# Attention's values projected first in each layer, and attention begun half a stretch earlier beside the last pairs' scan

## The chip, the cores and the metric

The kernel runs on one core of a Trainium2 chip. The metric is the device time of one execution in microseconds (us); the median of three runs is given. A profile is of one execution, whose span runs from its first to its last instruction.

## The reference

Two layers of a bidirectional encoder, 256 tokens of width 2048 in float32. Each layer normalises its input, makes one wide projection, and feeds two groups: a bidirectional RWKV-7 scan (16 heads of 64, one scan forward and one backward) and windowed attention (16 query heads, 4 key and value heads of 64, with rotary positions and a sink). Both are gated, joined, projected back and added to the input.

```python
h = rms_norm(x, norm_g[l])
proj = h @ w_in[l]
rw_in, g_rw, q, k_at, v_at, g_at = split(proj)
rw_in = bidir_token_shift(rw_in, shift_mu[l])
r, k, v, xw, xa = split(rw_in)          # xw, xa: low-rank inputs of decay and in-context rate
y_rw = rwkv7_branch(r, k, v, xw, xa, ...)   # both directions summed, normed, plus a bonus term
y_at = window_attention(rope(q), rope(k_at), v_at, sink[l])
mix = concat([y_rw * silu(g_rw), y_at * silu(g_at)])
x = x + mix @ w_out[l]
# after both layers: rms_norm(x, final_g)
```

## The kernel before

**The stream.** Every projection runs as a queue of *steps*, in an order written out by hand (class `Stream`, `S.add` and `S.run`). A step is three matmuls of 128x128 against 128x256 (lines 311 to 313): weights and activations are each split into a high part (float32r) and the rest, and high by high, high by low and low by high are summed. The activations of a layer lie in `XH` and `XL`, 16 slices (`k`) of 128 rows; `x_split` makes a slice's two parts, one on ScalarE (L203), one on VectorE (L204). A weight tile of 512 KB (`raw`, three buffers) serves eight steps; it is loaded by SP's queue (L233) and split into `hi` on ScalarE (L241) and `lo` on VectorE (L243), two buffers of each, asked for two steps before its first step. A projection's 128 columns are 16 steps into one accumulator (`pm`); two such buffers exist (`ps_main`). When it is full, its `evac` function is emitted; `S.later(n, f)` emits `f` n steps later.

**Order of the stream in a layer, 864 steps.** The low-rank inputs `xw` and `xa` (32 steps), eight pairs of RWKV heads with k, v, r and gate (512), attention's values (32: `v_step`, tokens as the stationary side, two accumulators of 128 tokens by 256 columns, both in `ps_main`), attention's two key tiles (32), and queries and gates of eight head pairs (256). After that come 256 steps of the output projection.

**Stretches.** `window(64, ...)` emits 64 steps in 11 groups; before each group it lets the generators that are listed for this group go one piece further: `scan_p` (preparation), `scan_i` (a triangular inverse), `scan_b` (the chain over four chunks) of the pairs at that lag, `setup_` (constants, the rotary sine and cosine; layer 0 only) and `attend`. So the pieces' small matmuls stand between stream steps in TensorE's order, which is the program's. The other engines' instructions are ordered by a scheduler at compile time, by priorities. Stretch w works on pairs w to w-4. Each layer has 13 stretches (numbered from 0); 32 steps run ahead of the first of them, in layer 0 while x arrives (one step for each slice of x, then 16 more) and in layer 1 behind layer 0's output projection.

**Attention.** `attend` has 16 pieces and a rest: `scores(j)` (12 matmuls into `pscr`, softmax on VectorE and ScalarE), `flip(j)` (transposes of the probabilities), `values(j)`. Table `ATT` says in which groups of the last three stretches a piece stands; the last of these has no scan.

**Buffers touched.** `S` of scores: tag `mv`, or `ge` for j = 2. Keys' low halves: tags `kd` and `kkr`. `VA` holds the values, and in layer 0's setup the rotary angles. `FR` (tag `s0b`) is scan_p's. `lead` does not exist yet; the low-rank projections use `ps_main` (in layer 0 the first uses a bank of the pair pool `ps_w`).

Of the kernel before, what the change touches and what calls it, by code (L numbers as in the profile page):

```python
# [9 lines left out]
F32 = mybir.dt.float32  # L10
# [11 lines left out]
T = 256  # L22
# [24 lines left out]
STAGE_I = (list(range(SLOTS)), [0, 1, 2, 3, 4])  # L47
STAGE_B = (list(range(5, SLOTS)), [i for i in range(SLOTS) if i != 7], [7])
ATT = [
    [3, 9],  # L50
    [1, 3, 5, 6, 8, 10],
    [0, 2, 4, 5, 6, 8, 9, 10],
]

ROT = {0: [2, 3], 1: [], 7: [2, 5, 7], 8: [1, 3], 9: []}
# [78 lines left out]
def hybrid_trunk_kernel(ctx, tc, xT, wi, wv, wo, par, fing, dup, iup, sink, pos, cst, out):  # L134
# [21 lines left out]
    def wbank(name):  # L156
        return wpair(name)[:, 0]
# [160 lines left out]
        S.add(ld[0], [step(k) for k in range(8)])  # L318
        S.add(ld[1], [step(k) for k in range(8, 16)], lambda: evac(box[0]))

    first_w = [wrp.tile([128, 1024], F32, tag="raw", name="raw") for _ in range(2)]
    G0 = cp.tile([128, NKT], F32, name="G0")
    X0 = Rows("s0", F32, "X0")
    SY.dma_start(out=first_w[0][:, 0:512], in_=wi[0, 0, 0, :, 0:512])
    SY.dma_start(out=G0, in_=par[0, :, P_NG : P_NG + NKT])
    for a, b in ((0, 2), (2, 4), (4, 8), (8, 12), (12, 16)):
        SY.dma_start(out=X0[:, a:b, :], in_=xT[:, a:b, :])
        if a == 0:
            SY.dma_start(out=first_w[0][:, 512:1024], in_=wi[0, 0, 0, :, 512:1024])
        if a == 4:  # L330
            SY.dma_start(out=first_w[1], in_=wi[0, 0, 1])
    mhalf = cp.tile([128, 4], F32, name="mhalf")
    V.memset(mhalf, -0.5)

# [12 lines left out]
    def setup():  # L347
        posi = st("t1", [T], I32, bufs=3)
        SY.dma_start(out=posi, in_=pos.to_broadcast([128, T]))
        SY.dma_start(out=FG, in_=fing)  # L350
        SY.dma_start(out=SK, in_=sink.to_broadcast([128, DEPTH * 16]))
        cin = st("mv", [C_N - C_KEEP], bufs=3)
        SY.dma_start(out=cin, in_=cst[:, C_KEEP:C_N])
        for l in range(DEPTH):
            s = DP[:, l, 0:NSH]
            V.tensor_tensor(s, PR[:, l, P_MU0 : P_MU0 + NSH], PR[:, l, P_MU1 : P_MU1 + NSH], op=ALU.add)
            V.tensor_scalar(s, s, -1.0, 1.0, op0=ALU.mult, op1=ALU.add)
            h = DP[:, l, NSH : NSH + 8]
            V.tensor_scalar(h, PR[:, l, P_KA : P_KA + 8], 0.5, None, op0=ALU.mult)
            V.tensor_scalar(DP[:, l, NSH + 8 : NSH + 16], h, -1.0, 1.0, op0=ALU.mult, op1=ALU.add)  # L360
            V.tensor_scalar(DP[:, l, NSH + 16 : NSH + 32], PR[:, l, P_A0 : P_A0 + 16], 0.5, None, op0=ALU.mult)
        V.tensor_scalar(SK, SK, 8.0, None, op0=ALU.mult)
        yield

        V.tensor_copy(
            LV.rearrange("p l s (n x) -> p (l s) n x", x=32),
            cin[:, 512 : 512 + 64 * NL].rearrange("p (n x) -> p n x", x=32).unsqueeze(2).to_broadcast([128, 2 * NL, NC, 32]),
        )
        V.memset(MSK, 1.0)
        V.memset(MSK[:, :, 0:1], 0.0)  # L370
        V.tensor_copy(band, cin[:, 0:512])
        A.activation(BONES, ones, AF.Copy, scale=0.0)
        for r in half:
            A.activation(BONES[r, r], ones[r, r], AF.Copy)
        V.tensor_copy(EYE, cin[:, 512 + 64 * NL : 576 + 64 * NL])
        V.tensor_scalar(NEYE, EYE, -1.0, None, op0=ALU.mult)
        V.tensor_scalar(EYE2, EYE, 2.0, None, op0=ALU.mult)
        yield

        AN = st("VA", [2, T])  # L380
        ang, nn = AN[:, 0], AN[:, 1]
        V.tensor_copy(ang, posi)
        yield
        PV.tensor_scalar(ang, ang, C[:, C_OFF["inv"] : C_OFF["inv"] + 1], None, op0=ALU.mult)
        yield

        def reduce_by(dst, src, period, bits, shift):
            PV.tensor_scalar(nn, src, 1.0 / period, shift, op0=ALU.mult, op1=ALU.add)
            yield
            PV.tensor_scalar(nn, nn, MAGIC, MAGIC, op0=ALU.add, op1=ALU.subtract)  # L390
            yield
            cur = src
            for p in split_const(period, bits, 4):
                PV.scalar_tensor_tensor(dst, nn, -p, cur, op0=ALU.mult, op1=ALU.add)
                cur = dst
                yield

        two_pi = 2.0 * np.pi
        yield from reduce_by(ang, ang, two_pi * 4096.0, 7, 0.0)
        for dst, shift, add in ((SIN, 0.0, 0.0), (COS, 0.25, np.pi / 2)):  # L400
            yield from reduce_by(dst, ang, two_pi, 11, shift)
            if add:
                PV.tensor_scalar(dst, dst, float(add), None, op0=ALU.add)
            PV.tensor_scalar(dst, dst, PI_IN, -PI_IN, op0=ALU.min, op1=ALU.max)
            yield
        for dst in (SIN, COS):
            PA.activation(dst, dst, AF.Sin)
        yield
        PV.tensor_scalar(SIN, SIN, C[:, C_OFF["sgn"] : C_OFF["sgn"] + 1], None, op0=ALU.mult)
        yield  # L410
# [30 lines left out]
    def queue_inputs(l):  # L441
# [53 lines left out]
            A.activation(hi, x[0:rows], AF.Copy)  # L495
            V.tensor_tensor(lo, x[0:rows], hi.bitcast(F32), op=ALU.subtract)

        if l == 0:

            inproj(0, lambda pm: S.later(29, lambda: xw_evac(pm)), raws=first_w, bank=lambda: wbank("pm")[:, 0:T])  # L500
            inproj(1, lambda pm: S.later(13, lambda: xa_evac(pm)))
        else:
            inproj(0, xw_evac)
            inproj(1, xa_evac)


        L.ts = [dict() for _ in range(NP)]
# [60 lines left out]

            return evac

        pvs = []

        def v_step(kk, b):
            def f(w):
                if not pvs:
                    pvs.extend(ps_main.tile([128, T], F32, tag="m", name="pva") for _ in range(2))
                k = kk % 4
                wh, wl = (x[:, k * 256 : (k + 1) * 256] for x in w)
                tb = slice(b * 128, (b + 1) * 128)
                PE.matmul(pvs[b], L.XH[:, kk, tb], wh, start=(kk == 0), stop=False)  # L580
                PE.matmul(pvs[b], L.XH[:, kk, tb], wl, start=False, stop=False)
                PE.matmul(pvs[b], L.XL[:, kk, tb], wh, start=False, stop=(kk == 15))

            return f

        def v_evac():
            L.VA = st("VA", [2, 256])
            with tc.high_priority(offset=PRIO_B):
                A.activation(L.VA[:, 0, :], pvs[0], AF.Copy, scale=L.norm.rt[:, 0:1])
                V.tensor_scalar(L.VA[:, 1, :], pvs[1], L.norm.rt[:, 1:2], None, op0=ALU.mult)  # L590

        for qt in range(4):
            S.add(
                lambda qt=qt: wsplit(wload(wv[l, qt])),
                [v_step(qt * 4 + k, b) for k in range(4) for b in range(2)],
                v_evac if qt == 3 else None,
            )

        def k_place(m):
            def place():  # L600
                if m == 0:
                    L.KA = [st("KA", [2, T], F32R), [st(n, [T], F32R) for n in ("kd", "kkr")]]
                return L.KA[0][:, m, :], L.KA[1][m]

            return place
# [68 lines left out]
    def layer(l):  # L674
# [399 lines left out]
        def scores(j):  # L1074
            m, g = divmod(j, 4)
            t = L.tq[j]
            Sc = t["S"] = st("ge", [2, 2, 264], bufs=2) if j == 2 else st("mv", [2, 2, 264], bufs=3)
            ps2 = wpair("pscr")
            pss = [ps2[:, h] for h in range(2)]
            qh, ql = t["q"]  # L1080
# [49 lines left out]
        def attend():  # L1130

            scores(0)
            yield
            flip(0)
            scores(1)
            yield
            for x in (MH, ML):
                x.more()
            for j in range(8):
                values(j)  # L1140
                if j < 6:
                    scores(j + 2)
                yield
                if j < 7:
                    flip(j + 1)
                    yield

        for w in range(NP + 2):
            window(64, *scans(w), *([(setup_, ROT.get(w, [2, 5, 9, 9]))] if l == 0 else []))
        att = attend()  # L1150
        window(64, *scans(NP + 2), (att, ATT[0]))
        window(64, *scans(NP + 3), (att, ATT[1]))
        window(64, (att, ATT[2]))
        for _ in att:
            pass

# [10 lines left out]
    L0.XH, L0.XL = Rows("s2", F32R, "XH"), Rows("s3", F32R, "XL")  # L1167
    for k in range(NKT):
        x_split(L0.XH, L0.XL, X0[:, k, :], k, 0)
        S.run(1)  # L1170
    ACC = st("mv", [4 * T], bufs=3)
    for q in range(4):
        x4 = X0[:, 4 * q : 4 * q + 4, :].rearrange("p k t -> p (k t)")
# [2 lines left out]
        else:  # L1176
            SQ = st("mv", [4 * T], bufs=3)
            PA.activation(SQ, x4, AF.Square)
            PV.tensor_tensor(ACC, ACC, SQ, op=ALU.add)
    S.later(20, lambda: L0.norm.add([ACC[:, i * T : (i + 1) * T] for i in range(4)]))  # L1180
    S.later(27, lambda: L0.norm.spread())
    S.run(8)
    SY.dma_start(out=C, in_=cst[:, 0:C_KEEP])
    SY.dma_start(out=PR, in_=par.rearrange("l p n -> p l n"))
    setup_ = setup()
    next(setup_)
    S.run(8)
    for l in range(DEPTH):
        queue_output(l)
        if l + 1 < DEPTH:  # L1190
            queue_inputs(l + 1)
        layer(l)
        S.run(NKT * 16)
        if l + 1 < DEPTH:
            S.run(32)
    end.norm.add(end.sums)
    end.norm.spread()
    X2 = layers[-1].X2
# [86 lines left out]
```

## Time and profile before

| what | value |
|---|---|
| median of 3 runs | 1171.13 us (1170.99 to 1171.94) |
| profiled execution | 1172.07 us, span 1170.3 us, granted clock 0.994 |
| TensorE busy | 1147.2 us (98%) |
| VectorE busy | 907.0 us (78%) |
| ScalarE busy | 786.4 us (67%) |
| DMA | 166.63 MB, mean 142 GB/s |

The page's lines give for an engine its busy time; a timeline row has start, duration, engine, line, operation, `out<-in` tiles, shape, count, and in brackets the engine's idle time before it with what ended it. PE is TensorE, PEld its weight load, DVE VectorE, ACT ScalarE, POOL GpSimd, SP the engine that issues the DMAs. Matmuls are pipelined: their starts say more than their durations.

### The profile page before, as it was taken

To read this page: it belongs to the slowest core of one execution; us is meant where nothing else is said; L and a number is where in the kernel's file an instruction comes from. 1 tells how busy PE (TensorE), PEld (TensorE's weight loads), DVE (VectorE), ACT (ScalarE), POOL (GpSimd) and SP (SyncE) were. 2 spreads that over 40 slices of the span, in tenths; PEclk is the share of its full clock that TensorE was granted. 3 is DMA by queue.
4 is the path that set the end of the run, shared out by engine and by line. 5 is a ranking of instruction groups with operands and counts; after the bars stand their busy time and mean duration, and the time that the engine had idled before them with its cause. 6 is when DMAs were issued, how large, how long until landed. Compare 5 with 4: busy or idle time off the path is not lost.

```text
span 1170.3 us, 38097 instructions
## 1 busy us (share of the span) xinstructions
PE 1147.2 (98%) x16151; PEld 1073.1 (92%) x16151; DVE 907.0 (78%) x2017; ACT 786.4 (67%) x1987; POOL 21.8 (2%) x23
## 2 busy tenths in 40 slices
PE   8999999999999999999999999999999999999996
PEld 6998999999899989899999899999999999899996
DVE  6889978888877677766678888978887767786554
ACT  6667877786876666645556677876886666675552
POOL 0000000000000000000000000000000000000000
PEclk9999999999999999999999999999999999999998
DMA  7544333233333433477655443333333343336663
GB/s 261 167 153 133 125 105 130 100 105 112 105 125 116 135 118 128 141 228 241 210 184 173 134 135 116 111 113 121 98 111 111 123 143 114 118 132 203 207 191 120
DMA packets 60410, 166.63 MB, mean 142 GB/s; under 512 B 7728, under 2 KB 22736, under 8 KB 60240
## 3 DMA queue, kind: packets, MB, share of 16 engines
q1 hardware_dynamic: 60240, 164.21, 43.2%
q8 instruction: 126, 2.06, 0.7%
q14 instruction: 44, 0.36, 0.1%
HBM read 157.37 MB, written 4.19 MB: 138 GB/s over the span
## 4 chain that ended last, share of the span: by engine, by line
PE 75%; issue 13%; DVE 6%; ACT 3%; DMA 1%; SPq 0%; POOL 0%; POOLq 0%; DVEq 0%; ACTq 0%
PE pm L311 19%; PE pm L313 16%; PE pm L312 16%; PE pg L833 3%; DVE lo L243 2%; PE pcc L996 2%; PE pcc L1024 2%; PE pd L940 1%; PE py L1008 1%; PE py L981 1%; PE pq L931 1%; PE pcc L1014 1%; ACT hi L241 1%; DMA raw<-wi 1%; PE pza L691 1%
## 5 line engine op out<-in xcount | busy, mean ns | idle before, releaser
L243 DVE TENSOR_TENSOR lo<-raw,hi 128x512 fp32r<-128x512 f32 x560 | 372.4, 687 | 112.8 <-ACT hi L241 103.7
L241 ACT ACTIVATE hi<-raw 128x512 fp32r<-128x512 f32 x560 | 329.7, 625 | 167.6 <-PE pm L312 96.3
L311 PE MATMUL pm<-XHa,hi 128*128 128x256 f32 x832 | 246.9, 297 | 1.4 <-ACT XHa L203 0.8
L311 PE MATMUL pm<-XHb,hi 128*128 128x256 f32 x832 | 242.9, 292 | 0.2 <-ACT hi L241 0.2
L313 PE MATMUL pm<-XHb,lo 128*128 128x256 f32 x832 | 233.6, 281 | 2.4 <-DVE lo L243 2.4
L313 PE MATMUL pm<-XHa,lo 128*128 128x256 f32 x832 | 234.3, 282 | 1.2 <-DVE lo L243 1.0
L312 PE MATMUL pm<-XLa,hi 128*128 128x256 f32 x832 | 234.3, 282 | 0.5 <-DVE XLa L204 0.3
L312 PE MATMUL pm<-XLb,hi 128*128 128x256 f32 x832 | 233.5, 281 | 0.4 <-DVE XLb L204 0.4
L311 PEld LDWEIGHTS pm<-XHa,hi 128*128 128x128 f32 x832 | 157.2, 189 | 13.8 <-issue 3.2
L311 PEld LDWEIGHTS pm<-XHb,hi 128*128 128x128 f32 x832 | 156.5, 188 | 5.9 <-ACT hi L241 0.4
L313 PEld LDWEIGHTS pm<-XHa,lo 128*128 128x128 f32 x832 | 157.3, 189 | 2.5 <-DVE lo L243 2.5
L313 PEld LDWEIGHTS pm<-XHb,lo 128*128 128x128 f32 x832 | 156.6, 188 | 3.2 <-DVE lo L243 3.2
L312 PEld LDWEIGHTS pm<-XLa,hi 128*128 128x128 f32 x832 | 157.5, 189 | 1.1 <-DVE XLa L204 1.1
L312 PEld LDWEIGHTS pm<-XLb,hi 128*128 128x128 f32 x832 | 156.7, 188 | 0.6 <-DVE XLb L204 0.6
L1019 ACT ACTIVATE suv<-pcc 64x128 f32<-64x128 f32 x128 | 34.7, 271 | 71.0 <-PE pcc L1017 47.3
L311 PE MATMUL pm<-MHa,hi 128*128 128x256 f32 x256 | 72.0, 281 | 0.0
L313 PE MATMUL pm<-MHa,lo 128*128 128x256 f32 x256 | 71.7, 280 | 0.2 <-DVE lo L243 0.2
L312 PE MATMUL pm<-MLb,hi 128*128 128x256 f32 x256 | 71.6, 280 | 0.0
L313 PE MATMUL pm<-MHb,lo 128*128 128x256 f32 x256 | 71.6, 280 | 0.0
L312 PE MATMUL pm<-MLa,hi 128*128 128x256 f32 x256 | 71.6, 280 | 0.0
L311 PE MATMUL pm<-MHb,hi 128*128 128x256 f32 x256 | 71.6, 280 | 0.0
L311 PEld LDWEIGHTS pm<-MHa,hi 128*128 128x128 f32 x256 | 48.1, 188 | 0.9 <-issue 0.8
(293 smaller groups left out, 2325.1 us busy)
## 6 DMA issues: line engine op xcount, KB each, us to landing
raw<-wi SPq DMA_DIRECT2D x207, 512.0 KB
raw<-wo SPq DMA_DIRECT2D x64, 512.0 KB
raw<-wv SPq DMA_DIRECT2D x8, 512.0 KB
rrot<-u SPq DMA_DIRECT2D x80, 32.0 KB
vg<-xT SPq DMA_DIRECT2D x16, 128.0 KB
xd<-vg SPq DMA_DIRECT2D x16, 128.0 KB
vg<-xd SPq DMA_DIRECT2D x16, 128.0 KB
g<-dup SPq DMA_DIRECT2D x16, 97.0 KB
```

The source lines that it names most:

```text
L241: A.activation(hi[:, q], raw[:, q], AF.Copy)
L243: V.tensor_tensor(lo[:, q], raw[:, q], hi[:, q].bitcast(F32), op=ALU.subtract)
L311: PE.matmul(pm, wh, rh[:, kk, :], start=(kk == 0), stop=False)
L312: PE.matmul(pm, wh, rl[:, kk, :], start=False, stop=False)
L313: PE.matmul(pm, wl, rh[:, kk, :], start=False, stop=(kk == 15))
L691: PE.matmul(o, w[0], x[0], start=True, stop=False)
L833: PE.matmul(pg[:, h, c * 128 : (c + 1) * 128], BK[half[h], d, c, 1 - h : 3 - h, :].rearrange("p s j -> p (s j)"), MV[half[h], d, c].rearra ...
L931: PE.matmul(narrow(pq[:, d], h ^ d, c), hq(AB, d, c, h), sub(TC, h, d, c, d * b), start=True, stop=True)
L940: PE.matmul(narrow(pd[:, d], h, c), hx(TT, d, c, h), sub(QF, h ^ d, d, c, d * b), start=True, stop=True)
L996: PE.matmul(pc[half[h], 0, d, :], GE[h][r, d, ci[d], 0, :], SUV[r, d, ci[d], h, :], start=True, stop=True)
L1019: A.activation(here(h), pc[half[h], 1], AF.Copy)
L1024: PE.matmul(pS[half[h], d, :], BT[:, h, d, i, :], SUV[:, d, ci[d], h, :], start=(i == 0), stop=True, skip_group_check=True)
```

## The change

The values' 32 steps move from behind the pairs to the head of each layer's stream, ahead of `xw` and `xa`. In layer 0 they run with two steps for each arriving slice of x (a slice times two blocks of 128 tokens), in layer 1 block by block within a weight tile; three weight tiles of the values are loaded ahead, between x's parts. `xw` and `xa` go to a pair of banks (`lead`) of the pool `ps_w` in both layers. 64 steps instead of 32 run ahead of a layer's first stretch; there are 12 stretches of 64 steps and one of 32 (five groups). Attention's pieces start in stretch 9 instead of 10, beside the scans of the last pairs. Some buffers get other tags, `flip(1)` and `scores(2)` share a piece, the constants' loads (`C`, `PR`) are issued inside the loop over the slices, and the timers of the norm and of the low-rank exits get other counts.

```diff
 ATT = [
-    [3, 9],
-    [1, 3, 5, 6, 8, 10],
-    [0, 2, 4, 5, 6, 8, 9, 10],
+    [9],
+    [1, 4, 8],
+    [0, 2, 3, 5, 6, 8, 9],
+    [0, 1, 2, 3, 4],
 ]
...
-    first_w = [wrp.tile([128, 1024], F32, tag="raw", name="raw") for _ in range(2)]
+    first_w = [wrp.tile([128, 1024], F32, tag="raw", name="raw") for _ in range(3)]
...
-    SY.dma_start(out=first_w[0][:, 0:512], in_=wi[0, 0, 0, :, 0:512])
+    SY.dma_start(out=first_w[0][:, 0:512], in_=wv[0, 0, :, 0:512])
...
-            SY.dma_start(out=first_w[0][:, 512:1024], in_=wi[0, 0, 0, :, 512:1024])
-        if a == 4:
-            SY.dma_start(out=first_w[1], in_=wi[0, 0, 1])
+            SY.dma_start(out=first_w[0][:, 512:1024], in_=wv[0, 0, :, 512:1024])
+        if a in (2, 4):
+            SY.dma_start(out=first_w[a // 2], in_=wv[0, a // 2])
...
-        AN = st("VA", [2, T])
+        AN = st("KA", [2, T])
...
-        if l == 0:
-
-            inproj(0, lambda pm: S.later(29, lambda: xw_evac(pm)), raws=first_w, bank=lambda: wbank("pm")[:, 0:T])
-            inproj(1, lambda pm: S.later(13, lambda: xa_evac(pm)))
-        else:
-            inproj(0, xw_evac)
-            inproj(1, xa_evac)
+        pvs = []
...
+        turns = [(k, b) for k in range(4) for b in range(2)] if l == 0 else [(k, b) for b in range(2) for k in range(4)]
+        done = (lambda: S.later(23, v_evac)) if l == 0 else v_evac
+        raws = first_w if l == 0 else []
+        for qt in range(4):
+            S.add(
+                lambda qt=qt: wsplit(raws[qt] if qt < len(raws) else wload(wv[l, qt])),
+                [v_step(qt * 4 + k, b) for k, b in turns],
+                done if qt == 3 else None,
+            )
+
+        lead = []
+
+        def lead_bank(i):
+            def bank():
+                if not lead:
+                    lead.append(wpair("pm"))
+                return lead[0][:, i, 0:T]
+
+            return bank
+
+        inproj(0, (lambda pm: S.later(13, lambda: xw_evac(pm))) if l == 0 else xw_evac, bank=lead_bank(0))
+        inproj(1, (lambda pm: S.later(4, lambda: xa_evac(pm))) if l == 0 else xa_evac, bank=lead_bank(1))
...
-                    L.KA = [st("KA", [2, T], F32R), [st(n, [T], F32R) for n in ("kd", "kkr")]]
+                    L.KA = [st("KA", [2, T], F32R), []]
+                L.KA[1].append(st(("acc", "kd")[m], [T], F32R))
...
-            Sc = t["S"] = st("ge", [2, 2, 264], bufs=2) if j == 2 else st("mv", [2, 2, 264], bufs=3)
+            Sc = t["S"] = hold("s0b", F32, "S0", (2, 2, 264)) if j == 0 else st("mv", [2, 2, 264], bufs=3)
...
-                if j < 6:
+                if 0 < j < 6:
                     scores(j + 2)
                 yield
                 if j < 7:
                     flip(j + 1)
+                    if j == 0:
+                        scores(2)
                     yield
 
-        for w in range(NP + 2):
+        for w in range(NP + 1):
...
-        window(64, *scans(NP + 2), (att, ATT[0]))
-        window(64, *scans(NP + 3), (att, ATT[1]))
-        window(64, (att, ATT[2]))
+        for i in range(3):
+            window(64, *scans(NP + 1 + i), (att, ATT[i]))
+        window(32, (att, ATT[3]), groups=len(ATT[3]))
...
         x_split(L0.XH, L0.XL, X0[:, k, :], k, 0)
-        S.run(1)
+        S.run(2)
+        if k == 11:
+            SY.dma_start(out=C, in_=cst[:, 0:C_KEEP])
+            SY.dma_start(out=PR, in_=par.rearrange("l p n -> p l n"))
...
-    S.later(20, lambda: L0.norm.add([ACC[:, i * T : (i + 1) * T] for i in range(4)]))
-    S.later(27, lambda: L0.norm.spread())
+    S.later(18, lambda: L0.norm.add([ACC[:, i * T : (i + 1) * T] for i in range(4)]))
+    S.later(25, lambda: L0.norm.spread())
+    setup_ = setup()
     S.run(8)
-    SY.dma_start(out=C, in_=cst[:, 0:C_KEEP])
-    SY.dma_start(out=PR, in_=par.rearrange("l p n -> p l n"))
-    setup_ = setup()
     next(setup_)
-    S.run(8)
+    S.run(24)
...
-            S.run(32)
+            S.run(64)
```

More of the change, by code (lines that the diff above doesn't have):

```diff
@@ L496, in split, with v_step, f, v_evac @@
             V.tensor_tensor(lo, x[0:rows], hi.bitcast(F32), op=ALU.subtract)
-        if l == 0:
-            inproj(0, lambda pm: S.later(29, lambda: xw_evac(pm)), raws=first_w, bank=lambda: wbank("pm")[:, 0:T])
-            inproj(1, lambda pm: S.later(13, lambda: xa_evac(pm)))
-        else:
-            inproj(0, xw_evac)
-            inproj(1, xa_evac)
+        pvs = []
+        def v_step(kk, b):
+            def f(w):
+                if not pvs:
+                    pvs.extend(ps_main.tile([128, T], F32, tag="m", name="pva") for _ in range(2))
+                k = kk % 4
+                wh, wl = (x[:, k * 256 : (k + 1) * 256] for x in w)
+                tb = slice(b * 128, (b + 1) * 128)
+                PE.matmul(pvs[b], L.XH[:, kk, tb], wh, start=(kk == 0), stop=False)
+                PE.matmul(pvs[b], L.XH[:, kk, tb], wl, start=False, stop=False)
+                PE.matmul(pvs[b], L.XL[:, kk, tb], wh, start=False, stop=(kk == 15))
+            return f
+        def v_evac():
+            L.VA = st("VA", [2, 256])
+            with tc.high_priority(offset=PRIO_B):
+                A.activation(L.VA[:, 0, :], pvs[0], AF.Copy, scale=L.norm.rt[:, 0:1])
+                V.tensor_scalar(L.VA[:, 1, :], pvs[1], L.norm.rt[:, 1:2], None, op0=ALU.mult)
+        turns = [(k, b) for k in range(4) for b in range(2)] if l == 0 else [(k, b) for b in range(2) for k in range(4)]
[16 more added lines that the diff above has]
+        inproj(1, (lambda pm: S.later(4, lambda: xa_evac(pm))) if l == 0 else xa_evac, bank=lead_bank(1))
         L.ts = [dict() for _ in range(NP)]
@@ L569, in rope_evac @@
             return evac
[L571 to L597, printed above, removed]
         def k_place(m):
```

## The prediction

> **What bounds the kernel now.** I read the page's parts 1 and 2 first.
>
> ```profile
> span 1170.3 us, 38097 instructions
> PE 1147.2 (98%) x16151; PEld 1073.1 (92%) x16151; DVE 907.0 (78%) x2017; ACT 786.4 (67%) x1987; POOL 21.8 (2%) x23
> PE   8999999999999999999999999999999999999996
> PEclk9999999999999999999999999999999999999998
> ```
>
> TensorE is the bound: 1147.2 of 1170.3 us. The change neither adds nor removes a matmul, so what it can win is idle TensorE time, or time in which TensorE runs slowly. The busy time by 20 us stretches says where that lies.
>
> ```profile
> 0.00:20.00 20.00, 16.76 (x85) 12.42 (x85) 12.89 (x30) 15.01 (x28) 0.20 (x4) 0.91 0.77 273
> 20.00:40.00 20.00, 18.28 (x153) 17.86 (x153) 17.86 (x48) 11.92 (x25) 0.81 (x1) 1.00 0.56 190
> 60.00:80.00 20.00, 18.62 (x171) 17.87 (x172) 18.38 (x38) 14.84 (x35) 0.00 (x0) 1.00 0.55 179
> 1140.00:1160.00 20.00, 18.03 (x155) 17.86 (x153) 9.72 (x20) 9.15 (x18) 0.70 (x1) 0.98 0.25 80
> 1160.00:1180.00 20.00, 1.17 (x4) 0.88 (x4) 4.79 (x6) 0.38 (x1) 0.00 (x0) 0.69 0.27 105
> ```
>
> The first number after the length is TensorE's busy time. Of some 23 us of idle, 5.0 us (3.24 + 1.72) lie in the first 40 us and 11 us in the tail after the last projection, which the change does not touch. The first 20 us hold only 85 matmuls, the next 153: the opening is where TensorE does little, so I read its timeline.
>
> ```profile
> 1.22 4.57 PE L1164 MATMUL warm<-QF 128*128 128x512 f16 x11 [1.22 <-DVE QF L1159]
> 6.61 0.38 PE L311 MATMUL pm<-XHa,hi 128*128 128x256 f32 x1 [0.82 <-ACT XHa L203]
> 10.43 0.41 PE L311 MATMUL pm<-XHa,hi 128*128 128x256 f32 x1
> 10.64 0.41 PE L312 MATMUL pm<-XLa,hi 128*128 128x256 f32 x1
> 16.46 0.28 PE L311 MATMUL pm<-XHa,hi 128*128 128x256 f32 x1
> 19.75 0.39 PE L311 MATMUL pm<-XHb,hi 128*128 128x256 f32 x1 [0.18 <-ACT hi L241]
> 21.48 0.39 PE L313 MATMUL pm<-XHb,lo 128*128 128x256 f32 x1 [1.22 <-DVE lo L243]
> 21.71 0.28 PE L311 MATMUL pm<-XHb,hi 128*128 128x256 f32 x1
> 24.17 0.28 PE L311 MATMUL pm<-XHa,hi 128*128 128x256 f32 x1
> 25.59 1.84 PE L217 MATMUL pr<-C,mv 128*128 128x1 f32 x16
> 27.29 0.36 PE L311 MATMUL pm<-XHa,hi 128*128 128x256 f32 x1
> 29.69 0.39 PE L313 MATMUL pm<-XHb,lo 128*128 128x256 f32 x1 [0.50 <-DVE lo L243]
> 30.62 0.61 PE L227 MATMUL pr<-dg,C 128*128 128x128 f32 x4
> 30.98 0.36 PE L311 MATMUL pm<-XHb,hi 128*128 128x256 f32 x1
> ```
>
> A step of the stream is three matmuls (L311 to L313), so its L311 rows count the steps: 6.61 is step 0, 16.46 step 16, 21.71 step 25, 24.17 step 32. From step 25 to 32 a step costs 2.46/7 = 0.352 us. At 10.43 matmuls start 0.21 us apart, so a step costs 0.645 us; this half rate ends at about 12.2 us, by the starts in the timeline (the page's clock row, full but for the last slice, does not show it). Until 16.46 TensorE did 16 steps in 9.85 us, which at the full rate are 5.6 us: each arriving slice of x (k) feeds one step only. That is what the change's opening goes at.
>
> **The change, part by part.** I write T32 and T64 for the times at which steps 32 and 64 start.
>
> *Two steps for each slice of x (values first).* The values' matmuls have the shape of the others (128x256 moving), so a step is priced alike. Slices 0 to 3 fall into the half-rate time: slice 0 from 6.61, slice 1 after XLa at 8.44 (7.96 + 0.48, below), then 1.29 us a slice; by 12.2 some 8.5 steps are done. The other 23.5 at 0.352 us make 8.3 us: T32 = 20.5 if nothing else is late. What could be late is VectorE, which must make each slice's low part and each weight tile's:
>
> ```profile
> 7.96 0.48 DVE L204 SCALAR_TENSOR_TENSOR XLa<-X0a,G,XHa 128x256 fp32r<-128x256 f32 x1
> 8.66 0.89 DVE L204 SCALAR_TENSOR_TENSOR XLa<-X0a,G,XHa 128x256 fp32r<-128x256 f32 x2 [0.22 <-ACT XHa L203]
> 9.89 1.68 DVE L204 SCALAR_TENSOR_TENSOR XLa<-X0a,G,XHa 128x256 fp32r<-128x256 f32 x4 [0.35 <-ACT XHa L203]
> 11.61 1.29 DVE L243 TENSOR_TENSOR lo<-raw,hi 128x512 fp32r<-128x512 f32 x2
> 12.82 3.25 DVE L204 SCALAR_TENSOR_TENSOR XLb<-X0b,G,XHb 128x256 fp32r<-128x256 f32 x8
> 18.27 1.23 DVE L256 TENSOR_TENSOR mv<-mv 128x1024 f32<-128x1024 f32 x1 [1.00 <-ACT mv L256]
> 16.24 2.00 ACT L256 ACTIVATE mv<-X0a 128x1024 f32<-128x1024 f32 x2
> ```
>
> From 8.66 it has 0.89 + 1.68 + 3.25 of slices and three weight tiles of 1.29: 18.4 us, then the last slice's two steps, T32 = 19.2. So VectorE is just under TensorE's line. The transfers: 0.5 MB more (a third weight tile) stands between slices of x.
>
> ```profile
> 10.00:12.00 2.00, 2.00 (x11) 2.00 (x11) 1.97 (x5) 2.00 (x5) 0.00 (x0) 0.50 1.04 424
> ```
>
> At the 424 GB/s of this row (its last number) 0.5 MB is 1.2 us; slices 4 to 7, used from 9.35 on before (9.89 less the 0.5 us of their high part), come at about 10.6, TensorE wants them at 11.9: covered. With the cover gone (that DMA order slips by 2 us) T32 becomes about 22. I take T32 = 20.5, bounds 19.2 and 22.0; before 24.17.
>
> *From T32 to T64.* 32 steps are 11.3 us. The norm's small matmuls move with it (25.59 to 27.29 and 30.62 to 30.98: 2.06 us), 0.3 us of odd pitch as before. The squares of x (four of 1.0 us on ScalarE, three additions of 1.2 on VectorE) come right after slice 15 in both kernels and again stand 8 steps ahead of the next weight tile: before, the waits at 19.75 and 21.48 came of it. I take 1.2 us again; below, nothing if the scheduler slips the weights between them. The constants' load (cin) waits for a buffer of those squares and holds the weight loads behind it on SP's queue; before, that is the 0.50 at 29.69; now SP has the same order nearer to its need, I take 0.5, up to 1.8. T64 = 20.5 + 11.3 + 2.06 + 0.3 + 1.7 = 35.9.
>
> *Stretches shifted by 32 steps.* A stretch is 64 steps with one set of scan stages. Before, the first starts at 24.17, now at T64.
>
> ```profile
> 24.17:51.56 27.39, 26.89 (x228) 26.69 (x227) 21.88 (x60) 16.25 (x34) 0.81 (x1) 1.00 0.60 201
> 600.58:624.84 24.26, 24.26 (x208) 24.26 (x207) 17.06 (x33) 14.58 (x30) 0.00 (x0) 1.00 0.59 189
> 425.32:463.57 38.25, 38.25 (x384) 33.88 (x380) 28.71 (x92) 26.03 (x80) 1.01 (x1) 1.00 0.36 118
> ```
>
> These are layer 0's and layer 1's first stretch, and layer 0's with six attention steps beside the last pair's scan. Layer 1's first is free of the opening's work: 24.26. Layer 0's first now looks like that, with 0.2 us for setup: 24.5. So its end falls at 35.9 + 24.5 = 60.4 instead of 51.56, but 32 steps further (11.3 us): 2.5 us won. Pairs, their loads (iup, dup) and scans keep their places in the stretch, so later stretches cost what they did, without the values' steps. Those had four weight tiles in stretch 8; keys and queries with their rotations take the place there, and TensorE still bounds.
>
> *The values' exit.* Both accumulators sat in the projections' two buffers, and the next projection waited for the exit:
>
> ```profile
> 332.75 0.28 PE L582 MATMUL pva<-hi,XLb 128*128 128x256 f32 x1
> 333.23 0.39 PE L311 MATMUL pm<-XHa,hi 128*128 128x256 f32 x1 [0.21 <-ACT VA L589]
> 421.98 0.45 PE L1024 MATMUL pcc<-suv,bt 128*64 128x64 f32 x8
> 422.37 0.39 PE L311 MATMUL pm<-XHb,hi 128*128 128x256 f32 x1
> 424.70 0.45 PE L996 MATMUL pcc<-suv,ge 128*64 128x64 f32 x8
> ```
>
> Now the two low-rank projections behind it use a bank pair of their own: a start 0.48 us after the one before it becomes 0.12, 0.36 us a layer. In layer 1 the second accumulator is wanted four steps (1.4 us) after the last output tile; that tile's exit is 0.42 us on VectorE: hidden, up to 0.3 us lost if not.
>
> *Attention beside the scan.* From 421.98 to 424.70 lie six steps (2.11 us) and the small matmuls up to 422.37 (0.39), in 2.72 us: a break of the stream costs 0.2 us of its own. Attention steps that share a break with a scan step save most of it, I take 0.15. Before, 12 breaks a layer were attention's alone (three in stretch 11, eight in the last, one behind it), now 9 (three, five, one): 0.45 us a layer. The later buffers (S0 in FR's, keys' low halves in acc and kd) are free by then in program order, priced 0, 1 us at the most. KA for setup's angles is free until the keys: 0.
>
> **Sum**, against the profiled execution (1172.07 us; 0.94 above the median of 1171.13): opening 2.5, exits 2 x 0.36 = 0.7, breaks 2 x 0.45 = 0.9: 4.1 us. The median becomes 1167.0. With all bounds good (T32 19.2, no stall in the opening) the opening gives 5.6 and the sum 7.2: 1163.9. With T32 at 22.0 and 3.0 us of stalls it gives -0.2, the sum 1.4: 1169.7.
>
> **A rule on the clock.** The half rate lasts from the warm-up row at 1.22 (0.415 us for 512 columns, twice 0.21) to about 12.2. The Trainium skill, "TensorE: Matmul & The Clock Gate", Part 1, says that the clock is let go after one free-running busy window of about 3.4 us. The trace agrees only in part: 4.57 us of warm-up did not open it, the 3.5 us from 8.7 on did. By that rule the window's phase could keep the gate shut a window longer here; then 5.3 of the steps after 12.2 run at half rate, T32 is 22.0, and the time 1168.5.
>
> **The rivals.** (1) *The opening gives nothing.* VectorE is busy 17.86 of 20 us from 20 to 40: with values first, four more weight tiles' splits (5.2 us) come into the opening, and squares and additions hold them up; waits move from slices to weights. For it: the 1.22 and 0.50 us waits are of that kind. Against: until T64 the added work replaces evacuations and VectorE has a gap where TensorE lags. Opening between 0 and -1 us: 1169.7 to 1171. (2) *Slower: attention's softmax blocks the scan's last stages.* One scores step puts four exponentials of 0.50 us and their reads of 0.19 on ScalarE:
>
> ```profile
> L1102 ACT ACTIVATE mv<-mv,mx x56: 494/499/516, 401.3 to 1055.8; 128x257 f32<-128x257 f32 x56
> ```
>
> That is 2.8 us; the scan's copies (suv, 0.27) may queue behind, and TensorE, in order, then waits with the stream's matmuls behind it. Two more scores steps a layer stand beside the scan (seven for five); if these and their neighbours cost a full 2.8 us each, 4 x 2.8 = 11 us, 1178; it decides from 1.0 us a step. Against: the stretch from 425.32 has six attention steps beside the scan and TensorE is busy for 38.25 of 38.25. (3) *The gate stays shut longer*: worked out above, 1168.5, still a gain. (4) *Nothing happens to attention*: its steps stand at the same places of the stream (the first at step 692 for 689, the last at 857 for 858); it is the scans that come 32 steps later. Then only the 0.9 us are missing: 1167.9, inside the forecast.
>
> **How the numbers follow.** Forecast (1163.9 to 1168.4, point 1167.0) 0.62, with (4) in it; gate shut longer 0.08; opening worth nothing 0.17; slower 0.13. A measurement here can tell about 0.2%, 2.3 us, from no change, so faster means under 1168.8: 0.62 + 0.08 = 0.70; same 0.17; slower 0.13. The range runs from 1163.7 to 1170.3, which leaves out the slower case and some of each end.
>
> **What would show it.** Right: about 32 steps done by 20.5 us, the first stretch starting at 35 to 37, no wait of a projection for VA, stretches 1 to 8 as long as before, nine attention breaks a layer. Wrong: waits for lo or raw that sum to over 3 us before 40 us, or waits of pcc, ppt or pscr in stretches 9 to 11. Also wrong if layer 1 gains or loses more than 2 us, since I see only 0.8 there.

## The result, and the profile after

The changed kernel takes 1178.08 us (median of 6 runs, 1177.22 to 1180.36), the kernel before 1171.65 us on the same chip (6 runs, 1170.99 to 1173.43): ratio 1.0051, 95% interval 1.004 to 1.0061. It is slower by some 6 us, where 4 us less were forecast. The profiled execution took 1177.35 us, 5.3 more than that of before. The page's lines for the span and the engines:

```profile
span 1175.6 us, 38091 instructions
PE 1147.0 (98%) x16151; PEld 1073.5 (91%) x16151; DVE 908.2 (77%) x2017; ACT 785.0 (67%) x1987; POOL 22.0 (2%) x23
```

TensorE's busy time is what it was (1147.0 for 1147.2 us), so on the whole the 5.3 us are idle time; a matmul at half clock counts as busy. To find the places I cut both traces at the same steps of the stream, which the rows of L311 (now L312) and of the values' matmuls count. Half a stretch of the values moved from the end of a layer to its head; 32 steps at 0.352 us (11.27 us) are taken out of "after" in the openings and put back in stretches 8 to 12, so that like stands beside like.

| stage | before, us | after, us | difference |
|---|---|---|---|
| layer 0: start to the end of stretch 0 | 51.56 | 64.14 less 11.27 | +1.3 |
| stretch 1 | 28.67 | 29.26 | +0.6 |
| stretches 2 to 6 | | | -0.3 |
| stretch 7 | 41.75 | 43.30 | +1.55 |
| stretch 8 | 38.89 | 39.91 | +1.0 |
| stretches 9 to 12 | 144.24 | 132.02 plus 11.27 | -0.95 |
| output projection | 91.13 | 91.90 | +0.8 |
| layer 1: to the end of stretch 0 | 36.89 | 49.42 less 11.27 | +1.3 |
| stretches 1 and 2 | 62.09 | 62.53 | +0.4 |
| stretch 8 | 38.89 | 39.90 | +1.0 |
| stretches 9 to 12 | 144.13 | 131.99 plus 11.27 | -0.9 |

Attention beside the scan won (twice 0.9); nearly everything else lost. The opening of layer 0 was to win 2.5 us. The stretches' windows of the changed kernel show where TensorE (second number, busy time) or its clock (the number before the last two) fell short: the steps 32 to 64, then stretches 0, 7, 8 and the ones with attention. The last two rows are two microseconds inside stretch 7.

```profile
20.43:39.91 19.48, 15.98 (x119) 15.08 (x117) 12.96 (x28) 8.12 (x14) 1.08 (x1) 0.91 0.51 169
39.91:64.14 24.23, 24.23 (x208) 24.23 (x207) 17.58 (x35) 15.30 (x32) 0.00 (x0) 1.00 0.53 173
284.85:328.15 43.30, 41.54 (x752) 38.61 (x750) 35.54 (x75) 33.74 (x86) 1.31 (x1) 0.96 0.32 104
328.15:368.06 39.91, 38.57 (x739) 35.49 (x737) 31.56 (x68) 27.83 (x76) 1.37 (x1) 1.00 0.37 118
...
311.00:312.00 1.00, 1.00 (x7) 1.00 (x7) 0.95 (x3) 0.99 (x4) 0.00 (x0) 0.59 0.08 29
312.00:313.00 1.00, 1.00 (x6) 1.00 (x6) 0.94 (x3) 1.00 (x5) 0.00 (x0) 0.50 0.06 16
```

Step 32 starts at 20.43 (forecast 20.5), step 64 at 39.91 (forecast 35.9), and stretch 0 then takes 24.23 (forecast 24.5): all of the opening's miss lies between 20.43 and 39.91. TensorE's timeline there:

```profile
33.78 0.38 PE L314 MATMUL pm<-XHb,lo 128*128 128x256 f32 x1 [1.83 <-DVE lo L244]
34.66 1.23 PE L228 MATMUL pr<-dg,C 128*128 128x128 f32 x4 [0.50 <-DVE dg L223]
...
36.33 0.41 PE L312 MATMUL pm<-XHb,hi 128*128 128x256 f32 x1
36.54 0.41 PE L313 MATMUL pm<-XLb,hi 128*128 128x256 f32 x1
...
38.40 0.39 PE L312 MATMUL pm<-XHb,hi 128*128 128x256 f32 x1 [0.59 <-DVE u L454]
```

These three waits make 2.9 us (a fourth, 0.6 us for `lo`, lies before 28 us), and from 34 to 38.4 the matmuls start 0.21 us apart, not 0.12: half rate. The clock of 0.91 over the 19.48 us of the first window is 1.8 us lost, by an estimate; what the time is without it stands in experiment 5. VectorE's timeline and SP's queue say why `lo` was late:

```profile
32.10 0.96 DVE L366 CAST LV<-mv 128x1536 uint8<-128x1536 f32 x1 [4.95 <-DMA mv<-cst]
32.98 0.15 DVE L220 TENSOR_SCALAR rt<-pr 128x2 f32<-128x2 f32 x1
33.05 0.68 DVE L244 TENSOR_TENSOR lo<-raw,hi 128x512 fp32r<-128x512 f32 x1
34.32 0.48 DVE L223 TENSOR_SCALAR dg<-C,rt 128x128 f32<-128x128 f32 x2 [0.59 <-POOL rt L221]
```

```profile
20.54 0.42 SPq L550 DMA_DIRECT2D g<-iup  x1
21.01 0.35 SPq L550 DMA_DIRECT2D g<-dup  x1
23.63 3.77 SPq L354 DMA_DIRECT2D mv<-cst  x1
27.51 15.82 SPq L234 DMA_DIRECT2D raw<-wi  x5
```

VectorE stood still for 4.95 us, for a cast of constants (`LV`, read from `cin`, which shares tag `mv` with the squares of x). The scheduler had put that cast ahead of the norm's scale `rt` and of the next weight tile's `lo`. The load was late because its issue took SP's queue 3.77 us, behind the loads of the first pair's low-rank weights (`iup`, `dup`), and that issue itself began only at 23.63, when the last square had been added and its buffer was free. The same rows of the kernel before: issue 0.36 us, five microseconds after `dup`.

```profile
14.35 0.33 SPq L513 DMA_DIRECT2D g<-iup  x1
15.60 0.27 SPq L513 DMA_DIRECT2D g<-dup  x1
20.85 0.36 SPq L353 DMA_DIRECT2D mv<-cst  x1
```

During the 3.77 us the DMA engines moved next to nothing (last two numbers: share and GB/s):

```profile
24.00:26.00 2.00, 1.74 (x14) 1.74 (x15) 2.00 (x4) 1.00 (x2) 0.00 (x0) 1.00 0.07 24
26.00:28.00 2.00, 2.00 (x20) 2.00 (x19) 1.15 (x2) 0.97 (x2) 0.00 (x0) 1.00 0.07 22
```

A share of 0.07 is about one engine of 16, and 4 us at 23 GB/s are 92 KB: the 97 KB of `dup`, whose tile has 97 rows (96 and a bias row). The Trainium skill, "DMA: Bandwidth & Descriptors", section "Why a DMA increments its semaphore by 16 and not by 1", says that a DMA runs on the largest number of engines, up to 16, that divides the size of the outermost dimension on both of its sides. Here that is 97 on both, a prime, so by that rule it runs on one. The trace agrees with that.

### The profile page after: what moved, and what is told of

Its sections match the earlier page's. It is cut to its first block, busy times and chain, and to the rows that moved or that the text cites. A ratio compares the mean times of both kernels' runs of the same rounds, so it can differ in the third digit from the quotient of the medians.

```text
span 1175.6 us, 38091 instructions
## 1 busy us (share of the span) xinstructions
PE 1147.0 (98%) x16151; PEld 1073.5 (91%) x16151; DVE 908.2 (77%) x2017; ACT 785.0 (67%) x1987; POOL 22.0 (2%) x23
## 3 DMA queue, kind: packets, MB, share of 16 engines
q1 hardware_dynamic: 60240, 164.21, 43.2%
## 4 chain that ended last, share of the span: by engine, by line
PE 73%; issue 12%; DVE 7%; ACT 4%; DMA 3%; SPq 0%; POOL 0%; DVEq 0%; POOLq 0%; ACTq 0%
PE pm L312 18%; PE pm L314 16%; PE pm L313 16%; PE pg L843 3%; DVE lo L244 2%; PE pcc L1006 2%; PE pcc L1034 1%; PE py L1018 1%; PE pd L950 1%; ACT hi L242 1%; PE py L991 1%; PE pcc L1024 1%; PE pq L941 1%; PE pscr L1097 1%; PE po L1137 1%
## 5 line engine op out<-in xcount | busy, mean ns | idle before, releaser
L312 PE MATMUL pm<-XHa,hi 128*128 128x256 f32 x832 | 246.7, 297 | 0.6 <-ACT hi L242 0.6
L312 PE MATMUL pm<-XHb,hi 128*128 128x256 f32 x832 | 243.7, 293 | 0.6 <-DVE u L454 0.6
L312 PEld LDWEIGHTS pm<-XHa,hi 128*128 128x128 f32 x832 | 156.4, 188 | 13.8 <-issue 4.3
L312 PEld LDWEIGHTS pm<-XHb,hi 128*128 128x128 f32 x832 | 157.6, 189 | 6.1 <-DVE u L454 0.9
L312 PE MATMUL pm<-MHa,hi 128*128 128x256 f32 x256 | 72.1, 282 | 0.0
L312 PE MATMUL pm<-MHb,hi 128*128 128x256 f32 x256 | 71.7, 280 | 0.0
L312 PEld LDWEIGHTS pm<-MHa,hi 128*128 128x128 f32 x256 | 48.2, 188 | 0.9 <-issue 0.8
```

What stands on the lines that cost most here:

```text
L312: PE.matmul(pm, wh, rh[:, kk, :], start=(kk == 0), stop=False)
```

## The experiments

The theory (A): the opening's loss is the late `cin`, late because of `dup` and because it waits for a buffer of the squares. Its rival (B): VectorE and the weight tiles are too late whatever `cin` does. Beside these, smaller suspects: the pair of banks `lead` (one tile for two accumulators) and the keys' rotation in stretch 8. The medians of before were 1173.51 us beside the first four experiments and 1173.46 beside the others; ratios are to these. The changed kernel's own ratio is 1.0051 in the result and 1.0036 [1.0023, 1.0049] in experiment 5. The intervals of experiments 3 and 4 overlap the latter: there the rows and stages carry the argument, not the whole time.

**1. Constants in a buffer of their own.**

```diff
-        cin = st("mv", [C_N - C_KEEP], bufs=3)
+        cin = hold("s1b", F32, "cin", (C_N - C_KEEP,))
```

> The changed kernel, but the constants' tile (cin, 480 KB) has a buffer of its own (tag s1b, free until stretch 2), so that its load need not wait for a buffer of x's squares. Theory A (the opening's gain is given back because cin comes late: it stands behind the first pair's iup and dup on SP's queue, VectorE's cast of it stands ahead of the norm's scale and of the weights' low parts, TensorE waits and its clock falls to half): no wait of TensorE over 0.7 us between 26 and 39 us, no half rate there, step 64 at 36 to 37 us instead of 39.9, the whole 1174 to 1175.5. Rival (VectorE's and ScalarE's own work binds the opening, wherever cin stands): step 64 stays at 39 or later, the whole within 1 us of 1178.

Measured 1172.83 us (10 runs), ratio 0.9999 [0.9988, 1.001], less than the 1174 to 1175.5 expected. In SP's queue and VectorE's timeline:

```profile
15.61 0.43 SPq L354 DMA_DIRECT2D cin<-cst  x1
...
27.16 0.95 DVE L366 CAST LV<-cin 128x1536 uint8<-128x1536 f32 x1
```

The load now stands ahead of `iup` and `dup`, the cast waits for nothing, the 1.83 us wait and the half rate in the opening are gone, and step 64 starts at 36.18 instead of 39.91. One wait is left there, 1.00 us for `u` at 34.67 (experiment 3). A holds, B falls. Stretch 7 took 41.84 this time, which needs experiment 5.

**2. `dup` as 96 rows and one row.**

```diff
-  SY.dma_start(out=t[n][0:rows], in_=src[l, :, :, p * 128 : (p + 1) * 128].rearrange("d r c -> r d c"))
+  cols = slice(p * 128, (p + 1) * 128)
+  for r in (slice(0, RANK), slice(RANK, rows)):
+      if r.start < r.stop:
+          SY.dma_start(out=t[n][r], in_=src[l, :, r, cols].rearrange("d r c -> r d c"))
```

> The changed kernel, but dup's load of 97 rows is two: 96 rows and 1 row. Theory (a load of 97 rows runs on one DMA engine at some 20 GB/s for 4 us and holds up the next issue on SP's queue; the changed kernel puts cin right behind it): cin's issue takes under 0.6 us instead of 3.77, its data are there by 29 us instead of 32.0, step 64 at 36.5 to 37.5, the whole 1174.5 to 1176; and the issues of 2.6 to 3.3 us behind each pair's dup are gone. Rival (the issue is long for another reason, the row count is none): cin's issue stays over 3 us and the time within 1 us of 1178.

Measured 1170.51 us (10 runs), ratio 0.9976 [0.9966, 0.9985]. SP's queue and VectorE:

```profile
21.55 0.44 SPq L553 DMA_DIRECT2D g<-dup  x1
24.17 0.35 SPq L354 DMA_DIRECT2D mv<-cst  x1
...
27.89 0.96 DVE L366 CAST LV<-mv 128x1536 uint8<-128x1536 f32 x1 [0.20 <-DMA mv<-cst]
```

The constants' issue takes 0.35 us for 3.77, at nearly the same moment and from the same buffer; the cast waits 0.20 for 4.95; step 64 starts at 36.62. So it is the one-engine load that held the queue. Stretch 1 falls as well, to 28.33 (29.26) in layer 0 and 28.36 (28.89) in layer 1: the waits for `lo` there (0.60 and 0.53 us) are gone; in the changed kernel ScalarE had waited 1.09 us, at 77.02, for a weight tile loaded behind `dup`. The whole fell by more than the 2 to 3.5 us expected. Between the two profiles 3.3 us lie in the opening, 1.5 in the two stretches 1, and 1.7 in layer 0's output projection, which the theory does not explain; stretch 8 of layer 0 takes back 0.6.

**3. `xw` and `xa` in separate PSUM tiles.**

```diff
-                if not lead:
-                    lead.append(wpair("pm"))
-                return lead[0][:, i, 0:T]
+            return lambda: ps_c.tile([128, T], F32, tag="yc"[i], name="pm")
```

> The changed kernel, but xw and xa each have a PSUM tile of their own (the scan's two single banks, idle then) instead of the two halves of one pair tile. Theory (xa's matmuls wait for the read of xw's half, because both halves are one tile): the waits of 0.6 us at 38.4 (on u) and at 611.2 are gone, 0.7 to 0.8 us each, the whole 1176.3 to 1177. Rival (they wait for weights, or for VectorE in general): both waits stay, no change.

Measured 1175.62 us (10 runs), ratio 1.0023 [1.0011, 1.0034]. What it takes away is, in the changed kernel, the wait in layer 1's TensorE timeline between `xw`'s last step and `xa`'s first; the first row is VectorE's read of `xw`:

```profile
610.65 0.42 DVE L454 TENSOR_TENSOR u<-pm,rb 128x256 f32<-128x256 f32 x1 [0.97 <-PE pm L314]
...
611.22 0.36 PE L312 MATMUL pm<-XHa,hi 128*128 128x256 f32 x1 [0.61 <-ACT hi L242]
```

The profile names `hi`, but the matmul starts 0.15 us behind the end of the read of the other half (611.07). With the halves apart that wait is gone, and steps 32 to 48 of layer 1 take 5.63 us for 6.41. They take 6.41 in all five profiles of the changed kernel that have the pair and 5.63 to 5.64 in the three that do not. In layer 0 the wait for `u` is gone too, but half clock fell differently into steps 48 to 64 (11.93 us for 12.96), so this pair of profiles does not give its cost there; experiments 1 and 2, without half clock, have a wait of 1.00 us, experiment 6 has none. The bank pair, which I had counted as a gain only, costs 0.8 us in layer 1 and, by those, about 1.0 in layer 0: `xa`'s first matmul waits until `xw` has been read, though it writes another bank.

**4. The second key tile's rotation two steps later.**

```diff
-                S.later(13, turn)
-                S.later(15, parts)
+                S.later(13 + lag, turn)
+                S.later(15 + lag, parts)
```

`lag` is 2 for the second key tile and 0 elsewhere.

> The changed kernel, but the second key tile's rotation is emitted two steps later, so that it stands behind the last pair's bonus low part on VectorE instead of ahead of it. Theory (the keys, moved into stretch 8 where the values stood, put four VectorE instructions ahead of that low part, and TensorE waits 1.2 us for it in both layers): stretch 8 takes 38.6 to 38.9 us instead of 39.9 in both layers, the whole 1175.8 to 1176.5. Rival (stretch 8 is longer by its own matmuls): 39.9 stays, no change.

Measured 1176.67 us (10 runs), ratio 1.0029 [1.0019, 1.0039]. The changed kernel's stretch 8 in layer 1, VectorE and the wait of TensorE:

```profile
928.08 0.42 DVE L257 TENSOR_TENSOR u<-u,TW 128x256 f32<-128x256 f32 x1
928.42 0.42 DVE L257 TENSOR_TENSOR rrot<-rrot,XA 128x256 f32<-128x256 f32 x1
929.36 0.42 DVE L257 TENSOR_TENSOR u<-u,rrot 128x256 f32<-128x256 f32 x1
930.26 0.42 DVE L257 TENSOR_TENSOR kd<-u,KA 128x256 fp32r<-128x256 f32 x1 [0.48 <-ACT KA L257]
931.40 0.42 DVE L257 TENSOR_TENSOR ip<-th,ip 128x256 fp32r<-128x256 f32 x1
...
931.87 0.39 PE L716 MATMUL pbn<-ip,BONES 128*128 128x256 f32 x1 [1.17 <-DVE ip L257]
```

The same matmul with the rotation later:

```profile
929.72 0.38 PE L716 MATMUL pbn<-ip,BONES 128*128 128x256 f32 x1 [0.24 <-DVE ip L257]
```

The key's rotation (the first four rows) stood in VectorE's order ahead of `ip`, the low part of the last pair's bonus, and one of its operations waited 0.48 us for ScalarE. TensorE waited 1.17 us for `ip` in this layer, 1.16 in the other. With the rotation later the waits are 0.23 and 0.24, and stretch 8 takes 39.49 (39.91) and 39.02 (39.90), not the 38.6 to 38.9 expected: that is nearly the whole loss of layer 1 and less than half of layer 0's. In layer 0 a wait of TensorE for the scan's `suv` grew from 0.18 to 0.42 us instead.

**5. The changed kernel once more.**

> The changed kernel as it is, beside the others of this group, as their measure. 5 to 6.5 us slower than before. A second thing to see: in stretch 7 the rotary sine's table load holds TensorE up for 1.8 us in every kernel; if the half rate behind it is a matter of the clock gate's phase, as I hold, it may come or not in the same program (stretch 7 then takes 43.3 or 41.8 us); if it belongs to the program, it comes again, 43.3.

Measured 1178.05 us (7 runs), ratio 1.0036 [1.0023, 1.0049]. Stretch 7 has a stall in every kernel here, while ScalarE makes setup's sine; in the changed kernel's first profile and in this one:

```profile
309.67 0.30 PE L950 MATMUL pd<-QF,tt 64*64 64x32 f16 x16 [1.76 <-ACT tt L912]
```

```profile
309.78 0.30 PE L950 MATMUL pd<-QF,tt 64*64 64x32 f16 x16 [1.76 <-ACT tt L912]
```

The second execution's windows behind that stall, and behind a wait in layer 1:

```profile
310.00:314.00 4.00, 4.00 (x93) 3.70 (x83) 3.08 (x9) 3.95 (x13) 0.00 (x0) 1.00 0.28 110
...
660.00:664.00 4.00, 2.94 (x15) 2.79 (x14) 3.45 (x6) 0.79 (x3) 0.00 (x0) 0.67 0.79 252
```

The same program, the same stall of 1.76 us: the first time half clock followed and the stretch took 43.30 us, this time not, and it took 41.81. This time half clock followed a wait of 1.06 us at 661.21 instead, and layer 1's stretch 1 took 30.35 for 28.89. So whether half clock comes behind a stall differs between executions of one program. Of the ten profiled executions of this study, five show it in stretch 7 (the changed kernel's first, experiments 2, 3, 4 and 7: 43.2 to 43.3 us) and five do not (41.7 to 41.8).

The opening is the more telling case. This execution has no half clock there (1.00, the number before the last two), and still:

```profile
21.17:39.75 18.58, 14.69 (x119) 13.88 (x117) 12.88 (x28) 8.01 (x14) 1.08 (x1) 1.00 0.51 170
...
34.01 0.38 PE L314 MATMUL pm<-XHb,lo 128*128 128x256 f32 x1 [1.25 <-DVE lo L244]
38.23 0.39 PE L312 MATMUL pm<-XHb,hi 128*128 128x256 f32 x1 [1.56 <-DVE u L454]
```

Steps 32 to 64 take 18.58 us at full clock, for 19.48 with half clock. The waits make 3.9 us here: at half rate TensorE comes later to `u` and waits 0.59 us for it, at full rate 1.56. With `cin` in time, they take 15.7 (experiments 1 and 2). So the late `cin` alone costs 2.9 us of the opening, and half clock some 0.9 on top.

**6. All four repairs.** The edits of experiments 1 to 4 together.

> The changed kernel with all four repairs at once: cin's own buffer, dup in 96 rows and 1, xw and xa in tiles apart, the second key tile's rotation two steps later. If the four costs are apart: step 64 at 35.2 to 35.6 us, stretch 1 28.3, stretch 8 38.8 to 39.5 in both layers, 0.8 less in layer 1's opening; 8 to 9.5 us less than the changed kernel, 2.5 to 4 us under the kernel before. If they are one cost seen four times (what one wait gives up, the next takes): no more than 1 us under the better of the single ones (cin's or dup's).

Measured 1167.55 us (5 runs), ratio 0.995 [0.9938, 0.9962]: faster than both kernels, 5.9 us below before and 10.5 below the changed kernel of experiment 5. Both are more than expected (2.5 to 4 and 8 to 9.5). Stretch 8 still takes 39.75 us in layer 0, over the 38.8 to 39.5 expected and the 38.89 of before. The page, and the windows up to step 64 and of stretch 0:

```profile
span 1165.1 us, 38126 instructions
PE 1142.5 (98%) x16151; PEld 1070.9 (92%) x16151; DVE 907.3 (78%) x2017; ACT 785.2 (67%) x1987; POOL 22.0 (2%) x23
```

```profile
0.00:35.45 35.45, 31.26 (x224) 28.08 (x225) 26.23 (x65) 23.62 (x45) 1.29 (x5) 0.95 0.75 257
35.45:59.70 24.25, 24.25 (x208) 24.25 (x207) 18.74 (x39) 15.61 (x33) 0.00 (x0) 1.00 0.58 194
```

Step 64 starts at 35.45 us, where the prediction had 35.9.

**7. The kernel before, with `dup` split.** The edit of experiment 2 in the kernel before.

> The kernel before with dup's load of 97 rows as 96 and 1, nothing else. Theory: in the kernel before, cin is issued 5 us after dup and hardly suffers, so only stretch 1's wait for a low part goes (0.3 to 0.5 us a layer) and the long issues behind dup: 0.5 to 1.5 us less than before. Rival (dup's trickle costs the kernel before as much as the changed one): 3 us less or more. Against the kernel with all four repairs this also says what the change itself is worth: I forecast 4.1 us before I knew of these costs, and expect 1.5 to 3 now.

Measured 1171.91 us (11 runs), ratio 0.9992 [0.9983, 1.0]; stretch 1 takes 28.34 us in both layers, 0.3 to 0.4 less. The one-engine load costs the kernel before 1.5 us by the medians, 0.9 by the ratio, whose interval just reaches no change: in its opening nothing that was wanted soon stood behind it. Against this kernel, experiment 6 is 4.4 us faster: that is what the change is worth with its side costs repaired, next to the 4.1 of the prediction's sum. (A buffer of its own for `cin`, whose cast waits 0.6 us in the kernel before, was not tried there.) The agreement is one of the sum. Against the kernel before, experiment 6's profile wins 3.1 us in layer 0's opening (2.5 forecast), 0.9 and 0.5 in stretches 9 to 12 and 0.9 in the output projection of layer 0; it loses 0.9 in that layer's stretch 8 and 0.2 in layer 1's opening.

**8. One step a slice again.** Experiment 6, with one step for each arriving slice and the 16 others behind.

```diff
-        S.run(2)
+        S.run(1)
...
-    S.run(24)
+    S.run(40)
```

> The kernel with all four repairs, but with one step for each slice of x instead of two (16 steps while x arrives, then 48 more before the first stretch); values still first. Theory (two steps a slice fill TensorE's gaps in the opening, and with the repairs the gain stays): step 32 at 23.5 to 24.5 us instead of 20.5, step 64 at 37.0 to 38.5 instead of 35.4, 1.6 to 3.1 us more than with all four. Rival (VectorE's and the transfers' total work sets step 64, however early TensorE starts): step 64 within 0.7 us of it.

Measured 1172.38 us (11 runs), ratio 0.9995 [0.9987, 1.0004], 4.8 us over experiment 6, more than the 1.6 to 3.1 expected. Step 32 starts at 26.27 (21.05 in experiment 6), step 64 at 39.86 (35.45).

```profile
20.19 0.38 PE L508 MATMUL pva<-hi,XHb 128*128 128x256 f32 x1 [2.46 <-ACT hi L242]
21.92 0.38 PE L509 MATMUL pva<-lo,XHb 128*128 128x256 f32 x1 [1.35 <-DVE lo L244]
...
20.00:24.00 4.00, 2.46 (x12) 2.27 (x13) 4.00 (x7) 3.47 (x8) 0.00 (x0) 0.80 0.26 97
24.00:28.00 4.00, 4.00 (x30) 4.00 (x29) 2.46 (x4) 1.15 (x2) 0.00 (x0) 0.77 0.74 226
```

Two steps a slice are where the opening's gain comes from. Of the 4.4 us that step 64 loses here, 1.7 are clock behind the two waits (0.20 and 0.23 of 4 us each), so the steps themselves are worth about 2.7 by these two profiles, an estimate near the 2.5 forecast. Experiment 6's own opening had half clock as well (0.95 over 35.45 us), but ahead of step 32, which all seven kernels with two steps a slice, with half clock there or without, start at 20.4 to 21.2 us.

## Why the prediction was wrong, point by point

**Two steps a slice: the gain right, the time of step 32 by luck.** Step 32 fell at 20.43 for 20.5, and by experiment 8 two steps are worth about the 2.5 us. But the prediction ran slices 0 to 3 at half rate up to 12.2 us, with 8.5 steps done by then. The changed kernel, from its first stream step to step 32, and the wait in it:

```profile
5.66:20.43 14.77, 13.21 (x96) 11.99 (x97) 13.29 (x36) 13.25 (x29) 0.00 (x0) 1.00 0.96 357
...
10.76 0.38 PE L508 MATMUL pva<-hi,XHa 128*128 128x256 f32 x1 [0.91 <-ACT XHa L204]
```

The clock is full throughout. Eight steps were done by 9.9 us; then TensorE waited for slice 4, which the prediction had called covered, and the other 24 took 9.67 us. A half rate that did not come and a wait that was not foreseen cancel. The rival with the gate shut longer did not come either.

The half rate in the kernel before was also misread. The prediction has it last from 1.22 to 12.2 us, not released by the warm-up. The clock in two windows of that trace:

```profile
6.00:8.00 2.00, 1.12 (x4) 0.67 (x4) 1.13 (x3) 1.54 (x3) 0.00 (x0) 1.00 0.97 351
9.00:12.00 3.00, 3.00 (x15) 2.82 (x15) 2.62 (x7) 2.67 (x7) 0.00 (x0) 0.50 1.03 422
```

When the first steps ran, the clock was full. Only at 8.8 us did it fall to half, and at 12.2 it came back.

**From T32 to T64: the step that failed.** The prediction had 15.4 us (35.9 less 20.5); it took 19.48. The term mis-sized is "now SP has the same order nearer to its need, I take 0.5, up to 1.8". I looked at whom the load of `cin` holds up on SP's queue and not at who waits for its data: the cast of `LV` holds VectorE, in order, and behind it stand `rt` and `lo`. Nor did I look at what stands ahead of it on the queue: before, `dup` was issued 5.25 us ahead of `cin`, now 2.6 us, so that its trickle (to about 27.4) fell on `cin`'s issue. The waits came to 3.5 us, a little over the 3.0 us of stalls that the prediction's bad end allowed. The half clock that followed them was in neither end; it is not what decides, since without it the 32 steps still took 18.58 us (experiment 5). With the late load gone (experiments 1, 2, 6) step 64 starts at 35.45 to 36.62.

**"A bank pair of their own", as a gain only: wrong.** The values' exit no longer holds the projections, as forecast, but the pair makes `xa` wait for the read of `xw`: 0.8 us in layer 1 and about 1.0 in layer 0 (experiment 3), more than the 0.36 won.

**"Later stretches cost what they did": wrong in stretch 8.** That TensorE bounds a stretch on the whole says nothing on a small operation that is wanted at one moment. The keys' rotation moved into the group of the last bonus and cost 1.0 us a layer net (the 0.36 of the exit is inside). Experiment 4 took back 0.9 and 0.4.

**Breaks: right in kind, twice the size.** Stretches 9 to 12 gained 0.95 and 0.87 us for 0.45. No wait for the scan's copies of weight came there (0.2 us in stretches 8 to 12 in all), so the rival of the softmax, whose time of 1178 the result has by chance, is wrong. I did not take apart why a shared break saves 0.3 us and not 0.15.

**Not in the sum at all.** Stretch 7's 1.55 us belong to the execution (experiment 5). The output projection of layer 0 was 0.8 us longer, and not by a wait: 16 steps take 5.70 us for 5.63 through most of it. It took 90.22 us in the three profiles of the changed kernel with `dup` split (experiments 2, 6 and 8) and 90.8 to 91.9 in the other seven, experiment 7 (91.25) among them. Why stays open.

**The rest.** "Waits for lo or raw that sum to over 3 us" was named as the sign of failure; the waits for `lo` made 2.8 us by then (0.35 at 17.58, 0.59 and 1.83). The sign came short because it left out the waits for `dg` and `u`, 1.1 us. "Layer 1 gains or loses more than 2 us" did not come: by the table it lost 1.8.

## What to carry to other kernels

When work moves ahead of a load, list for each queue what is now issued just before it, and for each engine what stands in order behind the first reader of its data; the second list was the dear one here. Price a wait with what the clock may do behind it: here half clock came behind 3.5 us of waits in one execution and not behind 3.9 us in another, and made 0.9 us of difference. Give a load a row count that spreads over the engines, and two accumulators that are read at different times two tiles.

## What the runs showed of the hardware

- A load of 97 rows ran at 22 to 24 GB/s on about one engine of 16 and kept the next DMA of the same queue in issue for 3.77 us; as 96 rows and one, that issue took 0.35 us. Such long issues stand behind other pairs' `dup` too.
- Half clock followed the stall of stretch 7 (1.76 to 1.79 us) in five of ten executions, and once a wait of 1.06 us; it lasted 3.4 us each time. It did not follow the waits of 1.25, 0.50 and 1.56 us in experiment 5's opening. The Trainium skill, "TensorE: Matmul & The Clock Gate", Part 1, has the clock fall after an idle window of about 3.4 us; these traces do not agree, since no such stall was that long. It also says that the window runs free of the program, and with that the differences between executions of one program (experiment 5) agree.
- A matmul into one half of a two-bank tile waited for a read of the other half (experiment 3). Whether the chip or the program's order asks for it was not told apart.
